# Opening of a two-layer encoder in a written order: low parts behind the next modulation, prompt's norm inside the first window of projections

## The chip, the cores and the metric

The kernel runs on one core of a Trainium2 chip. The metric is the device time of one execution in microseconds, the median of the runs shown.

## What is computed

Two token sequences, `sample` (512 tokens) and `prompt` (256 tokens), go through the same two layers with a model width of 1024. Each has its own conditioning vector `c`. The part that the change touches is the start of layer 0:

```python
def rmsnorm(x, g):
    xf = x.astype(jnp.float32)
    y = xf * lax.rsqrt(jnp.mean(xf * xf, axis=-1, keepdims=True) + EPS)
    return (y * g.astype(jnp.float32)).astype(x.dtype)
...
        mod = jax.nn.silu(c) @ adaln_w[l] + adaln_b[l]
        sh1, sc1, g1, sh2, sc2, g2 = [t[:, None, :] for t in jnp.split(mod, 6, axis=-1)]
        h = rmsnorm(x, norm_g[l, 0]) * (1 + sc1) + sh1
...
    proj = h @ w_in
```

`h` is projected onto the gates, queries, keys, values and output gates of a chunked mLSTM. Layer 1 has windowed attention in its place, and each layer ends with a convolutional feed-forward block. All matrix products are done to nearly full float32 precision.

## The kernel before

**Tiling.** Activations lie transposed: 8 chunks ("channels", `KC`) of 128 features on the partitions, 768 token columns. Columns 0 to 255 are prompt, 256 to 767 sample. `RANGES` cuts them into three ranges of 256 columns in the order sample, sample, prompt; `q` is 0 for sample and 1 for prompt.

**Split products.** A float32 operand becomes a high part (rounded to the type of one-pass products, by ScalarE, L232) and a low part (the rest, by VectorE, L233). A product is three products: high weight by high activation, high weight by low activation, low weight by high activation. Split activations live in `zh` and `zl` (also called `hh` and `hl`), split weights in `whi` and `wlo`, made from `raw`, a half unit of weights as loaded (128 x 1024). There are 5 buffers of `raw` and 3 each of `whi` and `wlo`.

**The opening.** `first` loads the x of the two sample ranges, computes the conditioning's first third (`adaln`, products of `silc` with rows of `adaln_w`) on TensorE and, meanwhile, the root mean squares of the two sample ranges (`Norm`, with `scaled` as what is done with the factors). Once shift and gain exist (L402, L405), `modulate` (L530 to L537) applies them to both ranges, channel by channel: gain and shift on VectorE (L534), then the split. `mlstm` then splits the first query weights, loads the x of prompt, squares it (L104, 8 tiles), and starts prompt's `Norm.stages`: first stage, sums over the squares by TensorE with two columns each (`pa<-inv,nt`, L120 region, recorded on the helper's line L226), epsilon on VectorE (L126), power on GpSimd (L127); second stage, factors spread over the partitions by TensorE (`pa<-kct,nr`), then `modulated` (L509): per channel a product on VectorE (L517), high part with shift on ScalarE (L519), low part on VectorE (L520).

**The window.** `window` (L283) takes three items (gates, first and second half of the first head's queries) and goes over the ranges in order; for each item it makes one tile of 24 products (8 channels by 3). After the second range, sample's results are evicted (`consume`: gates by L617 and L618, queries by L235 and L236), after the third, prompt's. `ready(rng)` makes sure that everything started for a range has been issued before the range is read; `tick` hands out dues of microseconds after which a started generator goes on.

**What sets the order.** The program is traced in the order of the code, and a planner reorders each engine's instructions by a simulated timeline. `manual_schedule(engines=...)`, used before only for the first feed-forward block, holds the instructions of its block on the named engines in traced order. DMAs are issued on SyncE's queue (SP). Passes for the conditioning of layer 1 (`adaln_v`, L474 and L476, tile `ada`) run on VectorE all through the mLSTM, as their rows arrive. After the window, the gates' rows go through logarithm and scans (L637 to L651), out to memory (`mrows`, L653) and back as masks and decays of the mLSTM.

Of the kernel before, what the change touches and what calls it, by code (L numbers as in the profile page):

```python
# [10 lines left out]
F32 = mybir.dt.float32  # L11
R = mybir.dt.float32r
AF = mybir.ActivationFunctionType
ALU = mybir.AluOpType
# [3 lines left out]
KC = D // P  # L18
# [4 lines left out]
SAMPLE, PROMPT = (256, 768, 0), (0, 256, 1)  # L23
RANGES = ((256, 512, 0), (512, 768, 0), PROMPT)
# [37 lines left out]
U_MIN = 0  # L62
# [22 lines left out]
class Norm:  # L85
# [11 lines left out]
    def x(self, c):  # L97
        return self.xt[c // 4][:, c % 4, self.rng[0] : self.rng[1]]
# [43 lines left out]
class Net:  # L142
# [137 lines left out]
            self.mm(o, wl[:, k], ah, False, k == KC - 1)  # L280
            yield o

    def window(self, items):  # L283

        bank = {}
        for rng in RANGES:
            self.ready(rng)
            c0, c1, q = rng
            s0, s1 = SEQS[q]
            for i, (w, consume) in enumerate(items):  # L290
                if (i, q) not in bank:
                    bank[i, q] = self.pa() if q else self.ps()
                wh, wl = (t.rearrange("p (k m) -> p k m", k=KC) for t in w)
                o = bank[i, q][:, c0 - s0 : c1 - s0]
                for k in range(KC):
                    ah, al = self.hh[:, k, c0:c1], self.hl[:, k, c0:c1]
                    self.mm(o, wh[:, k], ah, k == 0, False)
                    self.mm(o, wh[:, k], al, False, False)
                    self.mm(o, wl[:, k], ah, False, k == KC - 1)
                self.tick(2.6)  # L300
                if c1 == s1:
                    consume(q, bank[i, q][:, : s1 - s0])

    def gemmN(self, u, evac):

        ws = []
        for _, (hi, lo) in self.halves(u):
            ws.append((hi.rearrange("p (k m) -> p k m", k=4), lo.rearrange("p (k m) -> p k m", k=4)))
        for t in range(T // P):
            ps = self.ps()  # L310
            o = ps[:, :256]
            for k in range(KC):
                wh, wl = ws[k // 4]
                ah, al = self.hh[:, k, t * P : (t + 1) * P], self.hl[:, k, t * P : (t + 1) * P]
                self.mm(o, ah, wh[:, k % 4], k == 0, False)
                self.mm(o, al, wh[:, k % 4], False, False)
                self.mm(o, ah, wl[:, k % 4], False, k == KC - 1)
            evac(t, o)
# [208 lines left out]
            self.nc.vector.tensor_tensor(x(c), x(c), pr, ALU.mult)  # L527
        return ()

    def modulate(self, xt, rng, l, i):  # L530
        c0, c1, q = rng
        for c in range(KC):
            x = xt[c // 4][:, c % 4, c0:c1]
            self.nc.vector.tensor_scalar(  # L534
                x, x, self.gain[l][i][:, c, q : q + 1], self.mod[l][:, 24 * i + c, q : q + 1], ALU.mult, ALU.add
            )
            self.fp_copy_split(self.hh[:, c, c0:c1], self.hl[:, c, c0:c1], x)  # L537

    def output(self, x, pr, rng):
        nc = self.nc  # L540
# [63 lines left out]
    def mlstm(self, pool, gw, xt):  # L604
        nc, io = self.nc, self.io
# [14 lines left out]
        def keep(t, i, c):  # L620
            def evac(q, o):
                s0, s1 = SEQS[q]
                self.fp_copy_split(t[:, 0, c, s0:s1], t[:, 1, c, s0:s1], o, (1.0 / 16.0, None)[i])

            return evac

        qt0 = self.slab([P, 2, 2, T], R)
        ws = [(gw, gates)] + [(w, keep(qt0, 0, c)) for c, w in self.halves(U_MIN)]
        self.load_x(io["x"], RANGES[2:], xt)
        nc.sync.dma_start(self.kct[:, P:], io["kc"][:, P : 3 * P])  # L630
        norm = Norm(self, xt, PROMPT, self.modulated(0, 0), KC)
        for c in range(KC):
            norm.square(c)
        self.start(PROMPT, norm.stages())
        self.window(ws)
        nc.scalar.preload_act_table_set("natural_log_exp_and_others")
        nc.scalar.activation(ex, gf, AF.Abs)  # L637
        nc.scalar.activation(ex, ex, AF.Exp, scale=-1.0)
# [25 lines left out]
        for h in range(4):  # L664
# [48 lines left out]
            for q, (s0, s1) in enumerate(SEQS):  # L713
                n = (s1 - s0) // P
                for j in range(n):
# [7 lines left out]
                    w = (n + 1) * P  # L723
# [30 lines left out]
            for q, (s0, s1) in enumerate(SEQS):  # L754
                n = (s1 - s0) // P
                self.step(self.fillp, 2)
                hq = []
                for i in range(n):
# [5 lines left out]
                    for d in range(2):  # L764
                        o = self.pa()[:, :258]
                        js = range(0, i + 1) if d == 0 else range(i, n)
                        for j in js:
                            ph, pl = pts[q, j, d]
                            c0 = (i - j) * P if d == 0 else i * P
# [250 lines left out]
    def combined(self, l, i, pool):  # L1020
# [20 lines left out]
        def apply(x, pr, rng):  # L1041
            if rng[0] == 0:
                for c in range(KC):
                    full[c] = one(F32)
                    modulate(full[c], c, x, pr, rng)
                    put((self.B11, self.B21)[c // 4], c % 4, full[c])
                return
# [153 lines left out]
    def head(self, u0, last_tile, pool, urows, mark, early):  # L1201
# [48 lines left out]
        if not done:  # L1250
            self.fp_copy_split(*ahead[0], ah[0])
        first = self.outset(fixed(0), wa[0], rows[0][0])
        next(first)
        step()
        sums(1)
        wc[1] = self.split(ra[1])
        next(first, None)

        step()
# [181 lines left out]
    def first(self, pool):  # L1441

        x = self.io["x"]
        xt = self.load_x(x, RANGES[:1])
        ada = self.adaln(0, 0)
        steps = lambda n: [next(ada, None) for _ in range(n)]
        Norm(self, xt, RANGES[0], self.scaled).run()
        steps(4)
        self.load_x(x, RANGES[1:2], xt)
        steps(2)  # L1450
        Norm(self, xt, RANGES[1], self.scaled).run()
        self.graw = self.raw(self.io["wg"])
        steps(2)
        gates = self.split(self.graw)
        for rng in RANGES[:2]:
            self.modulate(xt, rng, 0, 0)

        def chain(*gens):
            for g in gens:
                yield from g  # L1460

        self.fillp = chain(*(self.adaln_g(0, grp) for grp in range(2, 6)))
        self.fill = self.adaln_v(1, pool)
        act = self.mlstm(pool, gates, xt)
        for _ in chain(self.fillp, self.fill):
            pass
        return act
# [129 lines left out]
```

## Time and profile before

| | |
|---|---|
| median of 3 runs | 1900.98 us (1899.35 to 1902.82) |
| the profiled execution's own time | 1904.33 us |
| its span in the profile | 1902.5 us |
| mean granted TensorE clock | 0.989 |
| TensorE busy | 1830.7 us, 96% of the span |
| VectorE, ScalarE, GpSimd busy | 1399.1, 910.3, 490.3 us |
| DMA | 184.48 MB, mean 97 GB/s |

PE is TensorE's products, PEld its weight loads, DVE VectorE, ACT ScalarE, POOL GpSimd, SP SyncE's queue. A row of the timeline gives start, duration, engine, line, operation, output and inputs, shape, count, and in brackets how long the engine was idle before and what released it. A busy TensorE is not TensorE at its peak: matmuls are pipelined, and their ends are modelled.

### The profile page before, as it was taken

What the parts mean: (1) busy time and instruction counts of PE and PEld (TensorE: products, weight loads), DVE (VectorE), ACT (ScalarE), POOL (GpSimd) and SP (SyncE); (2) the same over time, 40 slices, a digit from 0 to 9 for tenths busy, and PEclk for the clock granted to TensorE, in tenths of its full rate; (3) what the DMA queues carried; (4) which work ended last, traced back from release to release, by engine and by line L of the source; (5) the groups of instructions that cost most, each with busy time, mean ns of one, the idle gap of its engine ahead of it and who ended that gap; (6) DMA issues with size and microseconds to landing.
All of it is one profiled execution on the core that took longest, in us unless ns stands there. A gap on an engine that the chain in (4) does not pass through costs nothing. (4 is left out here: it accounts for less than half of the span.)

```text
span 1902.5 us, 29053 instructions
## 1 busy us (share of the span) xinstructions
PE 1830.7 (96%) x11270; PEld 1667.5 (88%) x11270; DVE 1399.1 (74%) x2296; ACT 910.3 (48%) x1832; POOL 490.3 (26%) x387
## 2 busy tenths in 40 slices
PE   7999999999999999999999999999989999999997
PEld 4987887888998999999999998779979999999997
DVE  4665577686689777777777755875997777777776
ACT  3444433444455444444444555774565444444443
POOL 2101001031023333333332211340133333333322
PEclk9999999999999999999999999999999999999998
DMA  8343556556312222222223221122222222222211
GB/s 330 109 134 121 167 181 195 168 164 208 99 53 69 68 67 67 67 67 67 67 67 100 90 89 43 44 85 89 78 78 78 67 67 67 67 67 67 67 34 67
DMA packets 64245, 184.48 MB, mean 97 GB/s; under 512 B 6167, under 2 KB 23831, under 8 KB 64108
## 3 DMA queue, kind: packets, MB, share of 16 engines
q1 hardware_dynamic: 64108, 182.63, 29.6%
q8 instruction: 88, 1.44, 0.3%
q14 instruction: 49, 0.40, 0.1%
HBM read 176.17 MB, written 6.43 MB: 96 GB/s over the span
## 5 line engine op out<-in xcount | busy, mean ns | idle before, releaser
L232 ACT CAST whi<-raw 128x1024 fp32r<-128x1024 f32 x237 | 248.5, 1049 | 412.2 <-PE pa L226 197.9
L233 DVE TENSOR_TENSOR wlo<-raw,whi 128x1024 fp32r<-128x1024 f32 x237 | 325.2, 1373 | 123.9 <-ACT whi L232 122.8
L226 PE MATMUL pa<-slab,whi 128*128 128x256 f32 (+1 forms) x1472 | 348.8, 334 | 4.7 <-DVE slab L557 4.5
L226 PEld LDWEIGHTS pa<-slab,whi 128*128 128x128 f32 x1472 | 254.0, 191 | 31.6 <-DVE slab L557 6.4
L557 DVE SCALAR_TENSOR_TENSOR slab<-pa,mod,slab 128x256 f32<-128x256 f32 (+1 forms) x368 | 207.6, 591 | 72.7 <-PE pa L226 72.3
L226 PE MATMUL pa<-slab,wlo 128*128 128x256 f32 (+1 forms) x736 | 235.4, 332 | 0.0
L226 PE MATMUL ps<-zh,whi 128*128 128x256 f32 (+2 forms) x688 | 228.8, 336 | 4.6 <-ACT whi L232 3.5
L226 PE MATMUL ps<-zh,wlo 128*128 128x256 f32 (+2 forms) x688 | 229.1, 336 | 4.0 <-DVE wlo L233 4.0
L226 PE MATMUL ps<-zl,whi 128*128 128x256 f32 (+2 forms) x688 | 229.4, 335 | 0.4 <-DVE zl L520 0.4
L1114 PE MATMUL ps<-zh,whi 128*128 128x384 f32 x504 | 171.1, 339 | 15.8 <-ACT ps L1169 14.5
L1115 PE MATMUL ps<-zl,whi 128*128 128x384 f32 x504 | 169.7, 337 | 0.8 <-DVE zl L1072 0.8
L1116 PE MATMUL ps<-zh,wlo 128*128 128x384 f32 x504 | 168.9, 335 | 0.0
L226 PEld LDWEIGHTS pa<-slab,wlo 128*128 128x128 f32 x736 | 140.2, 191 | 13.4 <-DVE wlo L233 0.9
L226 PEld LDWEIGHTS ps<-zh,whi 128*128 128x128 f32 x688 | 132.0, 193 | 17.5 <-ACT whi L232 5.1
L226 PEld LDWEIGHTS ps<-zh,wlo 128*128 128x128 f32 x688 | 132.2, 192 | 15.1 <-DVE wlo L233 4.8
L226 PEld LDWEIGHTS ps<-zl,whi 128*128 128x128 f32 x688 | 132.2, 193 | 11.5 <-issue 1.7
L1367 POOL TENSOR_TENSOR slab<-slab 128x772 f32<-128x772 f32 x44 | 83.7, 1903 | 205.0 <-DVE slab L1341 193.5
L1145 POOL TENSOR_TENSOR raw<-raw,raw 128x512 f32<-128x512 f32 x40 | 52.3, 1308 | 293.9 <-DVE wlo L233 244.3
L1340 DVE SCALAR_TENSOR_TENSOR slab<-slab,cstt,slab 128x771 f32<-128x771 f32 x88 | 104.8, 1193 | 26.9 <-ACT slab L1338 26.9
L1341 DVE SCALAR_TENSOR_TENSOR slab<-slab,cstt,slab 128x771 f32<-128x771 f32 x88 | 120.2, 1365 | 0.8
L476 DVE SCALAR_TENSOR_TENSOR ada<-raw,silc,ada 128x1024 f32<-128x1024 f32 x84 | 112.4, 1369 | 7.7 <-DMA raw<-in_adaln_w_dram 7.5
L1114 PEld LDWEIGHTS ps<-zh,whi 128*128 128x128 f32 x504 | 94.6, 188 | 23.9 <-ACT ps L1169 19.7
(291 smaller groups left out, 4155.0 us busy)
## 6 DMA issues: line engine op xcount, KB each, us to landing
raw<-in_w_dram SPq DMA_DIRECT2D x208, 512.0 KB, 3.7
raw<-in_adaln_w_dram SPq DMA_DIRECT2D x84, 512.0 KB, 4.3
slab<-in_x_dram SPq DMA_DIRECT2D x12, 512.0 KB, 7.6
slab<-in_adaln_w_dram SPq DMA_DIRECT2D x12, 512.0 KB, 10.3
slab<-mrows SPq DMA_DIRECT2D x8, 384.0 KB, 5.7
xs<-slab SPq DMA_DIRECT2D x6, 512.0 KB, 3.7
bt<-brow SPq DMA_DIRECT2D x16, 192.0 KB, 3.1
slab<-xs SPq DMA_DIRECT2D x6, 512.0 KB, 9.0
```

Source lines behind the costliest of these rows:

```text
L226: self.nc.tensor.matmul(out, lhsT, rhs, start=start, stop=stop)
L232: nc.scalar.copy(hi, src)
L233: return nc.vector.tensor_tensor(lo, src, hi.bitcast(F32), ALU.subtract)
L476: stt(acc[:, s], row, w, acc[:, s], ALU.mult, ALU.add)
L557: self.nc.vector.scalar_tensor_tensor(x, o, self.mod[l][:, gc + c, q : q + 1], x, ALU.mult, ALU.add)
L1114: mm(o, wh[:, k], hi[k], start=start and k == 0, stop=False, skip_group_check=True)
L1115: mm(o, wh[:, k], lo[k], start=False, stop=False, skip_group_check=True)
L1116: mm(o, wl[:, k], hi[k], start=False, stop=k == 3, skip_group_check=True)
L1145: tt(q[0], q[2], q[0], ALU.subtract)
L1340: stt(y[:, 1:], u[:, :-1], w(0), y[:, 1:], ALU.mult, ALU.add)
L1341: stt(y[:, :-1], u[:, 1:], w(2), y[:, :-1], ALU.mult, ALU.add)
L1367: nc.gpsimd.tensor_tensor(y, y, yrow[:, j], ALU.mult)
```

## The change

Prompt's norm and the window become one written section. `modulate` issues each channel's low part after the next channel's modulation, and calls `between(c)` after each high part: for the first range that is prompt's square of the same channel. The second range's modulation comes after the two weight splits. `window` takes prompt's stages: the sums are issued after the first tile, the factors and prompt's modulation after the fourth. The epsilon of prompt's mean is added by ScalarE (`last=True`, L124) instead of VectorE. TensorE, ScalarE and VectorE keep this order; SP and GpSimd are left to the planner. The other call of `window`, in layer 1, passes no stages.

```diff
--- before.py
+++ after.py
@@ -280,10 +280,16 @@
             self.mm(o, wl[:, k], ah, False, k == KC - 1)
             yield o
 
-    def window(self, items):
+    def window(self, items, stages=iter(())):
+
 
         bank = {}
+        n = 0
+        next(stages, None)
         for rng in RANGES:
+            if n == 2 * len(items):
+                for _ in stages:
+                    pass
             self.ready(rng)
             c0, c1, q = rng
             s0, s1 = SEQS[q]
@@ -300,6 +306,9 @@
                 self.tick(2.6)
                 if c1 == s1:
                     consume(q, bank[i, q][:, : s1 - s0])
+                n += 1
+                if n in (1, 4):
+                    next(stages, None)
 
     def gemmN(self, u, evac):
 
@@ -527,14 +536,21 @@
             self.nc.vector.tensor_tensor(x(c), x(c), pr, ALU.mult)
         return ()
 
-    def modulate(self, xt, rng, l, i):
+    def modulate(self, xt, rng, l, i, between=lambda c: None):
+
+        nc = self.nc
         c0, c1, q = rng
-        for c in range(KC):
-            x = xt[c // 4][:, c % 4, c0:c1]
-            self.nc.vector.tensor_scalar(
-                x, x, self.gain[l][i][:, c, q : q + 1], self.mod[l][:, 24 * i + c, q : q + 1], ALU.mult, ALU.add
-            )
-            self.fp_copy_split(self.hh[:, c, c0:c1], self.hl[:, c, c0:c1], x)
+        x = lambda c: xt[c // 4][:, c % 4, c0:c1]
+        for c in range(KC + 1):
+            if c < KC:
+                nc.vector.tensor_scalar(
+                    x(c), x(c), self.gain[l][i][:, c, q : q + 1], self.mod[l][:, 24 * i + c, q : q + 1], ALU.mult, ALU.add
+                )
+                nc.scalar.copy(self.hh[:, c, c0:c1], x(c))
+                between(c)
+            if c:
+                hi, lo = self.hh[:, c - 1, c0:c1], self.hl[:, c - 1, c0:c1]
+                nc.vector.tensor_tensor(lo, x(c - 1), hi.bitcast(F32), ALU.subtract)
 
     def output(self, x, pr, rng):
         nc = self.nc
@@ -625,14 +641,16 @@
             return evac
 
         qt0 = self.slab([P, 2, 2, T], R)
-        ws = [(gw, gates)] + [(w, keep(qt0, 0, c)) for c, w in self.halves(U_MIN)]
+        raws = [self.load(U_MIN, c) for c in range(2)]
         self.load_x(io["x"], RANGES[2:], xt)
         nc.sync.dma_start(self.kct[:, P:], io["kc"][:, P : 3 * P])
-        norm = Norm(self, xt, PROMPT, self.modulated(0, 0), KC)
-        for c in range(KC):
-            norm.square(c)
-        self.start(PROMPT, norm.stages())
-        self.window(ws)
+        norm = Norm(self, xt, PROMPT, self.modulated(0, 0), KC, last=True)
+        eng = mybir.EngineType
+        with self.tc.manual_schedule(engines={eng.PE, eng.Activation, eng.DVE}):
+            self.modulate(xt, RANGES[0], 0, 0, norm.square)
+            ws = [(gw, gates)] + [(self.split(raws[c]), keep(qt0, 0, c)) for c in range(2)]
+            self.modulate(xt, RANGES[1], 0, 0)
+            self.window(ws, norm.stages())
         nc.scalar.preload_act_table_set("natural_log_exp_and_others")
         nc.scalar.activation(ex, gf, AF.Abs)
         nc.scalar.activation(ex, ex, AF.Exp, scale=-1.0)
@@ -1452,8 +1470,6 @@
         self.graw = self.raw(self.io["wg"])
         steps(2)
         gates = self.split(self.graw)
-        for rng in RANGES[:2]:
-            self.modulate(xt, rng, 0, 0)
 
         def chain(*gens):
             for g in gens:
```

## The prediction

> **What bounds the kernel now.** The page of the profile comes first: the engines and the granted clock in 40 slices.
>
> ```profile
> PE 1830.7 (96%) x11270; PEld 1667.5 (88%) x11270; DVE 1399.1 (74%) x2296; ACT 910.3 (48%) x1832; POOL 490.3 (26%) x387
> PEclk9999999999999999999999999999999999999998
> ```
>
> TensorE holds 1830.7 of 1902.5 us; an edit of the opening pays only what it moves on TensorE's path, or what it moves on a chain TensorE later waits for. The change is in the first slice, 47.6 us long, and a little behind. So I cut that part into windows, then read it in order of time. The cut uses edges at which the granted clock changes (columns: length, busy time and count of PE, PEld, DVE, ACT, POOL, then clock, DMA share, GB/s):
>
> ```profile
> 34.79:38.20 3.41, 2.59 (x16) 1.95 (x15) 2.67 (x11) 2.96 (x10) 0.00 (x0) 1.00 1.03 410
> 38.20:41.61 3.41, 3.41 (x17) 3.41 (x17) 3.41 (x12) 3.41 (x10) 0.00 (x0) 0.50 0.88 350
> 41.61:45.03 3.42, 3.42 (x17) 3.42 (x18) 3.42 (x9) 3.30 (x9) 0.00 (x0) 0.50 0.05 18
> 45.03:48.44 3.41, 3.41 (x18) 3.41 (x18) 3.41 (x9) 0.00 (x0) 2.28 (x1) 0.50 0.51 154
> 48.44:51.85 3.41, 3.41 (x31) 3.41 (x31) 0.45 (x2) 0.00 (x0) 1.01 (x1) 1.00 0.46 154
> ```
>
> Half clock lasts from 38.20 to 48.44 us: 10.24 us, in which TensorE looks full. Timeline, TensorE:
>
> ```profile
> 25.09 1.50 PE L226 MATMUL pa<-inv,nt 128*128 128x2 f32 x12
> 35.37 1.30 PE L226 MATMUL pa<-inv,nt 128*128 128x2 f32 x8
> 36.84 0.38 PE L226 MATMUL ps<-zh,whi 128*128 128x256 f32 x1 [0.18 <-ACT zh L232]
> 37.87 5.16 PE L226 MATMUL pa<-inv,nt 128*128 128x2 f32 x24 [0.65 <-ACT nt L104]
> 42.89 0.56 PE L226 MATMUL ps<-zh,whi 128*128 128x256 f32 x1
> 44.53 0.41 PE L226 MATMUL ps<-zh,whi 128*128 128x256 f32 x1
> 45.17 0.41 PE L226 MATMUL ps<-zh,whi 128*128 128x256 f32 x1
> 51.27 0.60 PE L226 MATMUL pa<-kct,nr 128*128 128x128 f32 x4
> ```
>
> One product of the gates' tile runs at 36.84, then prompt's 24 remaining sums fill TensorE to 42.9; the rest of the 216 products follow. Prompt's factors slip in at 51.27. The three products of one channel take 45.17-44.53 = 0.64 us at half clock. VectorE, ScalarE and GpSimd in the same stretch:
>
> ```profile
> 26.86 0.72 POOL L127 TENSOR_TENSOR nr<-nr,mhalf 128x2 f32<-128x2 f32 x1 [1.83 <-DVE nr L126]
> 34.89 1.33 ACT L104 ACTIVATE nt<-slab 128x256 f32<-128x256 f32 x4
> 35.94 5.25 DVE L534 TENSOR_SCALAR slab<-slab,gain,mod 128x256 f32<-128x256 f32 x16
> 36.38 0.73 ACT L232 CAST zh<-slab 128x256 fp32r<-128x256 f32 x2 [0.16 <-DVE slab L534]
> 40.16 1.04 ACT L232 CAST whi<-raw 128x1024 fp32r<-128x1024 f32 x1
> 41.11 1.63 ACT L232 CAST zh<-slab 128x256 fp32r<-128x256 f32 x5
> 41.11 2.42 DVE L233 TENSOR_TENSOR zl<-slab,zh 128x256 fp32r<-128x256 f32 x7
> 43.46 1.21 DVE L233 TENSOR_TENSOR wlo<-raw,whi 128x1024 fp32r<-128x1024 f32 x1
> 46.16 3.29 POOL L127 TENSOR_TENSOR nr<-nr,mhalf 128x2 f32<-128x2 f32 x1 [18.59 <-DVE nr L126]
> 51.99 3.22 DVE L517 SCALAR_TENSOR_TENSOR nt<-slab,gain,pa 128x256 f32<-128x256 f32 x8 [3.10 <-issue]
> 52.50 3.31 ACT L519 ACTIVATE zh<-nt,mod 128x256 fp32r<-128x256 f32 x8 [7.59 <-DVE nt L517]
> 55.12 1.41 DVE L474 TENSOR_SCALAR ada<-raw,silc 128x1024 f32<-128x1024 f32 x2
> 56.45 3.25 DVE L520 SCALAR_TENSOR_TENSOR zl<-nt,mod,zh 128x256 fp32r<-128x256 f32 x8
> 57.43 0.69 ACT L617 ACTIVATE slab<-ps,cstt 36x512 f32<-36x512 f32 x1 [1.62 <-PE ps L226]
> 60.31 0.60 ACT L235 ACTIVATE slab<-ps 128x512 fp32r<-128x512 f32 x1 [1.49 <-PE ps L226]
> 60.45 2.48 DVE L476 SCALAR_TENSOR_TENSOR ada<-raw,silc,ada 128x1024 f32<-128x1024 f32 x2 [0.75 <-DMA raw<-in_adaln_w_dram]
> 63.19 0.60 ACT L235 ACTIVATE slab<-ps 128x512 fp32r<-128x512 f32 x1 [2.28 <-PE ps L226]
> 66.94 0.47 ACT L617 ACTIVATE slab<-pa,cstt 36x256 f32<-36x256 f32 x1
> ```
>
> Before, the planner runs all 16 modulations, then the low parts; and for prompt 8 products in a row, then the 8 low parts together. The tile evictions (57.43, 60.31, 63.19) show the pace of a tile of 24 products at full clock: 2.88 us, 0.36 per channel. Prompt's first tile thus starts at about 63.0 and ends at 65.9, unhindered: its last low part was done at 59.7.
>
> **First range and prompt's sums.** No instruction is added but one form of it: the epsilon goes from VectorE to ScalarE. The rest is order. VectorE now alternates modulation (5.25/16 = 0.33 us) and low part (2.42/7 = 0.35): 0.67 a channel. ScalarE alternates high part (1.63/5 = 0.33) and prompt's square (1.33/4 = 0.33): 0.66. From 36.38 the first channel, then seven steps of 0.67: the eighth low part ends near 41.8, and the gates' first tile on TensorE ends near 42.1. At half clock its products need 0.64 a channel, so VectorE is still the pace and the clock costs nothing here. Then the 32 sums stand alone on TensorE: 1.50/12 = 0.125 us each, 4.0 us, to 46.1. So 7.0 us of sums that lay over the modulation become 4.0 us that lie over nothing, and a tile of 2.9 takes their place; in exchange the products are no longer started at half clock.
>
> The two weight splits follow the first range on both engines (1.04 and 1.21 each): high parts 42.7 and 43.7, low parts 43.9 and 45.1, ahead of 46.1. The second range's modulation takes 8 x 0.67 = 5.4 us, to about 51. TensorE needs it from 46.1 + 2 x 2.88 = 51.9: hidden with 0.9 us to spare. The mean's epsilon now waits on ScalarE behind the last high part (50.7), and the power takes 0.72 us on GpSimd with VectorE idle, or up to 3.29 with VectorE busy as at 46.16: 51.4 to 54.0, against a need at 54.7. It is hidden, and its cover is thin. SP's queue gets the same loads in the same traced order: two weight halves, x of prompt, constants. I price that at nothing: the squares of before ran from 34.89 on, those of the written order from 36.7.
>
> **The fourth tile and prompt's factors.** The fourth tile's eviction falls at 46.1 + 3 x 2.88 = 54.7, against 57.43: 2.7 us ahead. The factors cost 0.6 on TensorE now instead of earlier: 2.1 ahead. Two tiles later, at 61.0, TensorE is at prompt's first tile, 2.0 us ahead of 63.0.
>
> But prompt's modulation starts only now, and in written order: product, high part, low part, next product. ScalarE first runs the gates' two evictions (0.69 for the one in the row above, L618's the same shape; to 56.1), which are queued ahead of the high parts. A channel then costs 0.51 from product to high part (51.99 to 52.50), 0.51 for a high part by itself (3.31 less seven steps of 0.40), and 0.40 from low part to next product (3.25/8): an estimate of 1.42 us. The first low part starts at 56.7, the eighth at 56.7 + 7 x 1.42 = 66.6 and ends at 67.1 (3.25 less seven steps is 0.45); the tile ends at 67.4. Unhindered it would have ended at 61.0 + 2.9 = 63.9: a wait of 3.5 us on TensorE is added, split over the last channels, with prompt's two other tiles queued behind it, and 2.0 ahead becomes 1.5 behind (65.9). Also behind that chain stand the evictions of the second and third sample tile, on ScalarE and VectorE; the banks that they free are wanted only after prompt's tiles. Below that, the price is nothing only if the low parts don't follow the written order (a rival below).
>
> Whether passes of the other layer's modulation (ada) slip into VectorE's gaps, the trace tells: an outsider does run inside a written section of the first feed-forward block, since L1340 stands ahead of L1317 of the section:
>
> ```profile
> 566.89 2.98 DVE L1340 SCALAR_TENSOR_TENSOR slab<-slab,cstt,slab 128x771 f32<-128x771 f32 x2
> 570.72 0.55 DVE L1317 TENSOR_TENSOR slab<-pa,nt 128x384 f32<-128x384 f32 x1
> ```
>
> The gap is 0.53 us; one of the two at 55.12 (0.7) costs 0.2, one of those at 60.45 (1.24) costs 0.7: 0 to 1.8 us for all four. I take 0, since the rows land when they do and VectorE is idle from 51 to 55, where the first pair fits.
>
> **What follows the opening.** These rows show who waits next:
>
> ```profile
> 85.82 0.38 SPq L653 DMA_DIRECT2D mrows<-slab  x1
> 88.81 0.43 SPq L241 DMA_DIRECT2D raw<-in_w_dram  x1
> 88.91 0.39 PE L226 MATMUL ps<-whi,zh 128*128 128x256 f32 x1 [0.46 <-DVE slab L233]
> 96.63 1.05 ACT L232 CAST whi<-raw 128x1024 fp32r<-128x1024 f32 x1 [7.75 <-DMA raw<-in_w_dram]
> 99.33 0.39 PE L226 MATMUL ps<-whi,zh 128*128 128x256 f32 x1 [1.52 <-DVE slab L233]
> ```
>
> A weight load at 88.81 stands on SP behind the gates' rows (85.82), these behind the scans, these behind prompt's gates (66.94): so the gates' date, and not TensorE's own lateness, sets 99.33. That tile ended at 65.9, and its eviction came 1.0 later, behind a weight split on ScalarE; that split (one of 1.04, like 40.16) becomes ready as the gates' tile ends. In the new order the date is 67.4 without it and 68.4 with it: 0.5 to 1.5 us later. I take 1.2, nearer the upper end, since the planner of before put the split first.
>
> **The clock.** The sums are work of two columns. In 38.20 to 41.61 they filled TensorE by the record (3.41 of 3.41) and the clock stayed at 0.50; it came back only after 45.03 to 48.44, which held products alone. The stretch that ended with half clock (34.79 to 38.20) held mostly such sums. So 4.0 us of sums between 42.1 and 46.1 may put the clock down again. If it drops as they end and one stretch of 3.41 us of products brings it back, the loss is 3.41/2 = 1.7 us; if it drops inside them, two stretches pass: 3.4 us; if an edge falls in their middle, both neighbours hold about half products: 0. I take the middle, 1.7.
>
> [...]
>
> The sum: +1.2 for the gates' date and +1.7 for the clock, +2.9 us on the profiled execution's 1904.33 (span 1902.5). That execution is 3.35 above the median of the runs, 1900.98; the difference goes onto the median: 1903.9 us. Its own bounds: 0.5 to 1.5 and 0 to 3.4, with ada 0 to 1.8, so +0.5 to +6.7.
>
> **The rivals.** *The clock stays up* (small sums count as work): the clock term is 0, +1.2 us, 1902.2. For it: 25.09, where twelve sums ran 0.125 each at full clock; against it: the 38.20 row. Within 0.2% as well.
>
> *The clock goes down for two stretches.* One mechanism: an edge of the windows falls in the last 1.5 us of the sums (44.5 to 46.1), half clock holds from there over the stretch that is part sums and over one whole stretch of products. Price 3.4 in place of 1.7, and the gates' tile ends after the split at the late end, 1.5: +4.9 us, 1905.9. With the edges of this execution (45.03) it is exactly this case. It decides as soon as the loss passes 3.8 - 1.2 = 2.6 us. One ada pair in the chain (1.4) does the same to a middle clock term.
>
> *The order isn't what is written, and the stage behind is planned anew.* If prompt's products still run first (3.22 in a row), the chain is short, the 2.0 us ahead stay; with the clock up and the load of 88.81 put ahead of the rows, the waits of 0.46 and 1.52 vanish too: -4.0 us, 1897.0. For it: a planner that orders by expected dates redoes everything after the opening. Against it: three conditions at once.
>
> **How the numbers follow.** 0.2%, 3.8 us, is about what a measurement of this kernel can tell from no change. Forecast (+2.9; its own range 1902 to 1904.8) 0.36, clock up 0.07, two stretches 0.35, planned anew and faster 0.22. Same is 0.43, slower 0.35, faster 0.22. The range takes the faster rival's 1897.0 as its low end, half of that case outside, and 1908.0 at the top (+6.7 is 1907.7): one in ten outside at each end.
>
> **What would show it.** Right: gates' first tile from 36.8 to about 42 at 0.66 a channel; 32 sums in one block behind it, some 4 us; prompt's VectorE row alternating L517 and L520 every 1.4 us or more; a TensorE wait of some 3.5 us in prompt's first tile on zl; its gates' eviction at 68 to 71; a second stretch of half clock between 43 and 52. Wrong: no such wait, or the full clock throughout after 41.6, or a difference that arises behind 100 us, by another order of loads and splits.

## The result, and the profile after

The changed kernel took 1910.82 us (median of 6 runs, 1907.03 to 1914.85) beside 1900.16 us for the kernel before (6 runs): a ratio of 1.0058, with a 95% interval of 1.004 to 1.0075. That is 10.7 us slower, and above the top of the predicted range (1908.0). A second set of six runs gave 1910.21 and 1.0054 (1.0036 to 1.0072).

The profiled execution took 1909.49 us, with a span of 1907.7. The page, engines and clock:

```profile
PE 1833.3 (96%) x11270; PEld 1667.3 (87%) x11270; DVE 1403.8 (74%) x2295; ACT 912.4 (48%) x1833; POOL 483.8 (25%) x387
PEclk9899999999999999999999999999999999999998
```

TensorE's busy time grew by 2.6 us, the span by 5.2. Only the second slice of the clock, 48 to 95 us, looks different. Windows of the profile after, cut at the edges at which the clock changes (columns as in the prediction):

```profile
37.79:41.21 3.42, 3.42 (x16) 3.34 (x16) 3.29 (x11) 3.42 (x12) 0.00 (x0) 0.51 0.97 387
41.21:44.62 3.41, 3.41 (x32) 3.40 (x31) 2.58 (x4) 1.92 (x3) 0.00 (x0) 1.00 0.14 25
44.62:48.03 3.41, 3.41 (x18) 3.41 (x18) 3.26 (x10) 1.94 (x5) 0.00 (x0) 0.50 0.85 275
48.03:51.44 3.41, 3.41 (x18) 3.41 (x18) 2.45 (x7) 0.68 (x2) 0.00 (x0) 0.50 0.05 22
...
65.09:68.51 3.42, 2.26 (x8) 1.25 (x8) 2.07 (x5) 1.17 (x3) 0.00 (x0) 1.00 0.24 93
68.51:71.92 3.41, 2.74 (x7) 1.69 (x7) 1.88 (x5) 1.50 (x4) 0.00 (x0) 0.50 0.00 0
71.92:75.34 3.42, 3.42 (x15) 3.18 (x16) 2.91 (x5) 3.25 (x6) 0.00 (x0) 0.50 0.00 0
75.34:78.75 3.41, 3.41 (x30) 3.41 (x30) 0.43 (x1) 3.36 (x4) 0.00 (x0) 1.00 0.51 159
```

Before, half clock ended at 48.44 and did not return in the opening. Now there are three spells: 3.4 us in the gates' first tile, 6.8 us from 44.62, the last part of the sums, on, and 6.8 us more, from 68.5, in prompt's tile: 17.1 us in place of 10.2. The stretch ahead of the third holds eight products (65.09).

TensorE's timeline after:

```profile
36.47 0.38 PE L226 MATMUL ps<-zh,whi 128*128 128x256 f32 x1 [1.36 <-ACT zh L549]
41.78 4.26 PE L226 MATMUL pa<-inv,nt 128*128 128x2 f32 x32
57.03 0.60 PE L226 MATMUL pa<-kct,nr 128*128 128x128 f32 x4
64.55 0.38 PE L226 MATMUL pa<-zh,whi 128*128 128x256 f32 x1 [0.43 <-ACT zh L528]
66.01 0.38 PE L226 MATMUL pa<-zh,whi 128*128 128x256 f32 x1 [0.43 <-ACT zh L528]
...
79.73 0.40 PE L226 MATMUL ps<-zh,whi 128*128 128x512 f32 x1
```

The 32 sums stand in one block. In prompt's first tile a product waits for each channel, 1.45 us apart. The last row is the first product with 512 columns behind the window, a mark that all kernels here share. In the kernel before it stands here:

```profile
71.63 0.40 PE L226 MATMUL ps<-zh,whi 128*128 128x512 f32 x1
```

The mark is 8.1 us later. VectorE after the change (L526 and L529 are the L517 and L520 of before, prompt's product and low part; L485 is the L476 of before, a pass of layer 1's conditioning):

```profile
49.06 1.42 DVE L483 TENSOR_SCALAR ada<-raw,silc 128x1024 f32<-128x1024 f32 x2 [0.96 <-DMA raw<-in_adaln_w_dram]
54.32 2.48 DVE L485 SCALAR_TENSOR_TENSOR ada<-raw,silc,ada 128x1024 f32<-128x1024 f32 x2 [1.63 <-DMA raw<-in_adaln_w_dram]
57.72 0.48 DVE L526 SCALAR_TENSOR_TENSOR nt<-slab,gain,pa 128x256 f32<-128x256 f32 x1 [0.92 <-issue]
59.04 0.48 DVE L529 SCALAR_TENSOR_TENSOR zl<-nt,mod,zh 128x256 fp32r<-128x256 f32 x1 [0.83 <-ACT zh L528]
59.44 0.47 DVE L526 SCALAR_TENSOR_TENSOR nt<-slab,gain,pa 128x256 f32<-128x256 f32 x1
60.69 2.48 DVE L485 SCALAR_TENSOR_TENSOR ada<-raw,silc,ada 128x1024 f32<-128x1024 f32 x2 [0.77 <-DMA raw<-in_adaln_w_dram]
63.09 0.48 DVE L529 SCALAR_TENSOR_TENSOR zl<-nt,mod,zh 128x256 fp32r<-128x256 f32 x1
63.48 0.47 DVE L526 SCALAR_TENSOR_TENSOR nt<-slab,gain,pa 128x256 f32<-128x256 f32 x1
...
64.94 0.47 DVE L526 SCALAR_TENSOR_TENSOR nt<-slab,gain,pa 128x256 f32<-128x256 f32 x1
65.99 0.48 DVE L529 SCALAR_TENSOR_TENSOR zl<-nt,mod,zh 128x256 fp32r<-128x256 f32 x1 [0.58 <-ACT zh L528]
...
71.80 0.48 DVE L529 SCALAR_TENSOR_TENSOR zl<-nt,mod,zh 128x256 fp32r<-128x256 f32 x1 [0.58 <-ACT zh L528]
```

Each low part waits 0.58 us for its high part, and the next product stands behind it. At 60.69 two ada passes have taken the gap between a product and its low part, 2.48 us long: from that product to the next are 4.04 us (59.44 to 63.48) in place of 1.46 (63.48 to 64.94). ScalarE, GpSimd and SP (L633 is the L617 of before, the gates' eviction; L671 its L653, the gates' rows):

```profile
52.38 0.87 POOL L127 TENSOR_TENSOR nr<-nr,mhalf 128x2 f32<-128x2 f32 x1 [25.18 <-ACT nr L124]
57.22 0.68 ACT L633 ACTIVATE slab<-ps,cstt 36x512 f32<-36x512 f32 x1 [4.92 <-PE ps L226]
73.95 0.47 ACT L633 ACTIVATE slab<-pa,cstt 36x256 f32<-36x256 f32 x1
92.77 0.37 SPq L671 DMA_DIRECT2D mrows<-slab  x1
```

Prompt's gates are evicted at 73.95, against 66.94: 7.0 us later. The rows follow at 92.77, 6.95 later.

Product by product, in the times of before, the profile after is behind by 8.0 us at 80, 5.1 at 120 to 140, 4.3 at 160 to 250, 7.1 around 300, 5.8 around 500, 6.2 at 1100 and 7.9 at 1800. The first part of the loss comes back where TensorE waited before: 2.3 us in three waits between 80 and 120, none of which is left. The profile of before then has a half-clock spell of 6.8 us at 1881 that the one after lacks, and the spans differ by 5.2. The order of the instructions behind the opening is nearly the same in both. The median gap of 10.7 is those 5.2, plus 4.2 by which the profiled execution of before was above the median of that set, plus 1.3 by which the one after was below its own.

### The profile page after: what moved, and what is told of

It is laid out like the page before. It is cut to its first block, busy times and chain, and to the rows that moved or that the text cites. A ratio compares the mean times of both kernels' runs of the same rounds, so it can differ in the third digit from the quotient of the medians.

```text
span 1907.7 us, 29049 instructions
## 1 busy us (share of the span) xinstructions
PE 1833.3 (96%) x11270; PEld 1667.3 (87%) x11270; DVE 1403.8 (74%) x2295; ACT 912.4 (48%) x1833; POOL 483.8 (25%) x387
## 5 line engine op out<-in xcount | busy, mean ns | idle before, releaser
L233 DVE TENSOR_TENSOR wlo<-raw,whi 128x1024 fp32r<-128x1024 f32 x237 | 331.8, 1401 | 122.3 <-ACT whi L232 121.1
L485 DVE SCALAR_TENSOR_TENSOR ada<-raw,silc,ada 128x1024 f32<-128x1024 f32 x84 | 108.9, 1326 | 7.6 <-DMA raw<-in_adaln_w_dram 7.5
```

Source lines behind the costliest of these rows:

```text
L233: return nc.vector.tensor_tensor(lo, src, hi.bitcast(F32), ALU.subtract)
L485: stt(acc[:, s], row, w, acc[:, s], ALU.mult, ALU.add)
```

## The experiments

Two theories stood at the start: the loss lies in the opening, as prompt's chain on VectorE and ScalarE, ada passes inside it and the clock's answer to the block of sums; or it arises behind it, by another plan of loads and splits. "Mark" below is the first product of 512 columns in the profiled execution; times are medians, and ratios are to the kernel before in the same set of runs. Where an expectation has a name for what sets the clock, the runs show of it the granted clock alone: 1.00 or 0.50, with edges on a grid of 3.41 us (last section).

**The changed kernel again.** No edit.

> The changed kernel once more, so that the experiments beside it are compared on one chip, and to see a second profiled execution. Theory (written chain and clock): the same picture in the opening, a wait of TensorE in prompt's first tile of about 5 us, half clock once around the sums and once in prompt's first tile, and a ratio of 1.004 to 1.007 to the kernel before. Rival (the 10.7 us of the medians are mostly an accident of the executions): a ratio near 1.003, as the one pair of profiles gives (1909.49 against 1904.33).

1910.21 us, mark 80.33, the same three half-clock spells 0.6 us later. The loss and its picture repeat.

**Prompt's low parts one channel behind.** In `modulated`:

```diff
+            late = []
...
-                nc.vector.scalar_tensor_tensor(lo, t, sh, hi.bitcast(F32), ALU.add, ALU.subtract)
+                late.append((lo, t, sh, hi.bitcast(F32), ALU.add, ALU.subtract))
+                if l or c:
+                    nc.vector.scalar_tensor_tensor(*late.pop(0))
+            for args in late:
+                nc.vector.scalar_tensor_tensor(*args)
```

> Prompt's low parts stand one channel behind the products in the written order, nothing else is changed. Theory (the strictly alternating chain of product, high part, low part holds up prompt's first tile): VectorE takes 0.8 us a channel instead of 1.45, the eighth low part ends near 65.5 instead of 72.3, prompt's first tile runs without a wait and near 66 its eviction begins, the half clock of 68.5 to 75.4 is gone, and TensorE is 6 to 8 us earlier behind the opening: a ratio of 1.000 to 1.002. Rival (the loss arises behind the opening, by another order of loads and splits): the opening is shorter, but the ratio stays at 1.004 or more.

1905.59 us, ratio 1.0026 (1.0015 to 1.0037). The timeline and one window of this kernel (an ada pair on VectorE, TensorE's wait, the window of prompt's tile, the mark):

```profile
62.05 2.48 DVE L485 SCALAR_TENSOR_TENSOR ada<-raw,silc,ada 128x1024 f32<-128x1024 f32 x2
66.56 0.39 PE L226 MATMUL pa<-zl,whi 128*128 128x256 f32 x1 [0.16 <-DVE zl L532]
65.08:68.50 3.42, 2.94 (x20) 2.31 (x19) 3.24 (x9) 2.29 (x5) 0.00 (x0) 1.00 0.51 153
74.89 0.40 PE L226 MATMUL ps<-zh,whi 128*128 128x512 f32 x1
```

A channel takes 0.79 us on VectorE, TensorE's waits fall to 0.16, the stretch at 65 holds 20 products in place of 8, and the half clock in prompt's tile is gone. The mark is 4.8 us earlier, although the first modulation came 1.3 us later in this execution (36.90 against 35.56); the median is 4.6 lower. An ada pair still stands in the chain (62.05), and the ratio is above the 1.000 to 1.002 that the theory gave. Of the causes tried singly, the low part that waits for its own channel's high part is the largest.

**The ada passes behind prompt's last low part.**

```diff
+                self.low = nc.vector.scalar_tensor_tensor(lo, ...)
...
-                        self.step(self.fill)
+                        with self.tc.issue_after(self.low.ins):
+                            self.step(self.fill)
```

> The passes for layer 1's conditioning that the planner slid into the section are queued behind prompt's last low part; the order of the section is kept as it is. Theory (the alternating chain, with the pair of passes of 2.48 us at 60.7 as its smaller part): the eighth low part ends some 2.5 us earlier, TensorE is 2.5 us earlier behind the opening, the wait in prompt's first tile stays at about 3 to 4 us: a ratio of 1.003 to 1.005. Rival (the pair of passes is what breaks the chain, and the alternation alone would be hidden): most of the loss goes, a ratio under 1.002.

1908.46 us, ratio 1.004 (1.0025 to 1.0056). The gates' eviction comes at 71.82, 2.1 earlier than after; the mark at 78.59, 1.1 earlier. So the pair does lie on the chain, but much of it is lost again by the mark. The intervals of the two kernels overlap, and its worth in time is not resolved.

**The sums in two halves,** 16 behind the first tile and 16 behind the second.

```diff
                 net.mm(pm[:, 2 * b : 2 * b + 2], ...)
+            if self.written and b < nb - 1:
+                yield 0.0
...
-                if n in (1, 4):
+                if n in (1, 2, 4):
...
+        norm.written = True
```

> Prompt's sums stand in two halves: 16 behind the first tile, 16 behind the second, instead of 32 behind the first; nothing else is changed. Theory (a stretch of 3.4 us that is mostly sums puts the clock down): with blocks of 2.1 us each stretch holds products for a third or more of its time, the clock stays up from 41 to 52, and the fourth tile is evicted 3.4 us earlier, near 53.8; the chain behind it moves with it, a ratio 0.0015 to 0.002 below that of the changed kernel. Rival (the clock comes back only after a fixed stretch of dense products from the start, however the sums stand): half clock from 44.6 to 51.6 as before, and the ratio of the changed kernel.

1914.36 us, ratio 1.0072 (1.0055 to 1.0089): by the medians slower than the kernel it was to mend, with overlapping intervals. The timeline of this kernel (L488 is the ada pass, L529 prompt's product, L636 the gates' eviction):

```profile
42.44 1.84 PE L229 MATMUL pa<-inv,nt 128*128 128x2 f32 x16
47.10 1.84 PE L229 MATMUL pa<-inv,nt 128*128 128x2 f32 x16
54.82 0.68 ACT L636 ACTIVATE slab<-ps,cstt 36x512 f32<-36x512 f32 x1 [2.14 <-PE ps L229]
55.67 2.48 DVE L488 SCALAR_TENSOR_TENSOR ada<-raw,silc,ada 128x1024 f32<-128x1024 f32 x2 [2.60 <-DMA raw<-in_adaln_w_dram]
58.07 0.47 DVE L529 SCALAR_TENSOR_TENSOR nt<-slab,gain,pa 128x256 f32<-128x256 f32 x1
61.64 2.48 DVE L488 SCALAR_TENSOR_TENSOR ada<-raw,silc,ada 128x1024 f32<-128x1024 f32 x2 [0.18 <-DMA raw<-in_adaln_w_dram]
```

The clock stays up from 42.1 to 66, and the fourth tile is evicted at 54.82, 2.4 earlier than after and where the prediction had put it. But the ada pair that came at 54.32 in the changed kernel comes at 55.67, now ahead of prompt's first product, and another stands within the chain. The gates' date is 73.45, the mark 79.85: the 2.4 us ended at a chain that did not move. The time is about 4 us above the changed kernel's, and a good part of that can be half clock: the granted clock is 0.9868 in the mean of these runs (each is listed to 0.001) against 0.9882 in those of the changed kernel beside them, 2.5 us if TensorE had work in all of it. The profile has longer spells (10.2 us at 66 and again at 151) and more of them behind 690. What brings them was not tested.

**The three together.** All three edits.

> The three edits together: low parts one channel behind the products in prompt's modulation, sums in two halves behind the first and second tile, the passes for layer 1's conditioning behind prompt's last low part. Theory (chain, passes and clock make up the loss in the opening): no wait in prompt's first tile, full clock from 42 on, the fourth tile evicted near 54.8, prompt's gates near 64 to 65 instead of 73.95, and the first 512-column product near 69.7, against 71.63 in the kernel before; a ratio of 0.998 to 1.000 if nothing else moves. Second theory (later waits of some 2 us, at the same places in every kernel, cost a half-clock stretch of 3.41 us, or 1.7 us of time, whenever one falls whole into a window of the monitor; a shifted opening chooses other hits): the opening as above, but the ratio anywhere from 0.997 to 1.004, with the difference to the opening's made up of half-clock stretches behind 100 us. Rival (another order of work behind the opening): a difference behind 100 us without half-clock stretches.

> The three changes together once more (low parts of prompt one channel behind, sums in two halves, layer 1's passes behind the last low part), as the base for the two kernels run beside it. Both theories expect what it gave: about 1900.7 us, ratio 1.000 to 1.002, the first product of 512 columns near 69 us, and half clock after the wait of 1.87 us near 676, because there the wait falls whole into one of the gate's stretches of 3.41 us.

1900.72 us, ratio 1.0008 (0.9999 to 1.0016), and in the second set 1901.12 us, 1.0016 (1.0005 to 1.0028). The mark is 68.91 and 69.54, ahead of the kernel before by 2.7 and 2.1. Mark and loss of the lead in the first set's profile:

```profile
68.91 0.40 PE L229 MATMUL ps<-zh,whi 128*128 128x512 f32 x1
87.55 0.84 ACT L779 ACTIVATE slab<-slab 36x768 f32<-36x768 f32 x1 [7.88 <-DVE slab L723]
88.92 2.75 PE L229 MATMUL pa<-slab,slab 128*128 128x512 f32 x6 [2.68 <-ACT slab L235]
```

Nearly all of the loss is undone by edits of the opening, so it came from there. The lead is gone by 90 us: TensorE waits 2.68 us for ScalarE's casts, which stand behind a step on the gates' rows (L779, at 87.55, before 86.81) that VectorE releases, and half clock follows at 89.2. Neither theory nor the rival had this wait. In the second set the profile has no half clock at 680, with a wait of 2.54 us in place of 1.87 and other edges: that spell is not a property of the kernel.

**The block alone.** The first two edits, the sums in one block.

> The three changes together but for the sums, which stay in one block behind the first tile: prices the block alone. Theory (the block puts the clock down for two stretches, 6.83 us at half speed, on TensorE's path): half clock from 44 or so to 51, the fourth tile's eviction near 57 in place of 54.3, the first product of 512 columns 3.4 us later, near 72.3, and 3 us on the time where later stretches are the same: 1902 to 1905. Rival (the loss is absorbed by prompt's chain, which has its own pace): the fourth tile late by 2.9, but the product of 512 columns near 70 and the time within 1 us of the base.

1904.28 us, ratio 1.0027 (1.0016 to 1.0038), 3.2 above the base of the same set. Windows and timeline of this kernel:

```profile
41.40:44.82 3.42, 3.42 (x32) 3.38 (x31) 2.59 (x4) 2.02 (x3) 0.00 (x0) 1.00 0.07 22
44.82:48.23 3.41, 3.41 (x17) 3.41 (x18) 3.26 (x11) 1.95 (x5) 0.00 (x0) 0.50 0.93 288
48.23:51.65 3.42, 3.42 (x18) 3.42 (x18) 2.23 (x7) 1.29 (x4) 0.87 (x1) 0.50 0.04 14
72.18 0.40 PE L226 MATMUL ps<-zh,whi 128*128 128x512 f32 x1
```

Half clock for two stretches, and the mark 2.6 to 3.3 later than with halves, near the 3.4 us that two half-clock stretches cost (6.83 us at a granted clock of 0.50): in the opening the block has that price when nothing slower stands behind it. On the time it is less sure: 3.2 us by the medians, 2.1 by the ratios, and the intervals overlap.

**No written window.** Only the modulations and splits are held in order; prompt's stages are started as before.

```diff
-            self.window(ws, norm.stages())
+        self.start(PROMPT, norm.stages())
+        self.window(ws)
```

> Only the modulations and weight splits stay a written section; prompt's stages are started as in the kernel before, and the planner places sums, factors and prompt's modulation around the window's tiles. Theory (the written places of prompt's norm are the fault, not the alternating modulation): half of the sums lie between the channels of the first tile, prompt's products stand eight in a row, no wait in prompt's first tile, at most one stretch of half clock after 41, and the first 512-column product near 67 to 69 against 71.63 before and 79.73 in the changed kernel; the ratio is below that of the changed kernel by 0.003 or more, 0.997 to 1.001 before later hits of the clock. Rival (the section itself, that is its modulations, is the fault): the ratio stays at 1.004 or more.

1902.0 us, ratio 1.0012 (1.0 to 1.0025). The planner puts 14 of the sums between the products of the first tile and the rest in two blocks behind it; half clock holds from 37.3 to 54.4, five stretches, and the mark is 75.17, not 67 to 69. Yet the median is below those of kernels with an earlier mark (1905.59 us with 74.89, 1904.28 with 72.18). One of its windows:

```profile
40.73:44.15 3.42, 3.42 (x18) 3.42 (x18) 2.45 (x6) 3.30 (x7) 0.00 (x0) 0.50 0.11 43
```

The ratio says that the written places of prompt's norm make most of the loss, and the written modulations alone do not. The mark is a guide to the opening, not a price in the total to the last 3 us.

**The kernel before, started later:** 14 small VectorE steps ahead of its first modulation.

```diff
+                for _ in range(7):
+                    g = self.gain[l][0][:, :, s]
+                    nc.vector.tensor_scalar(g, g, 1.0, None, ALU.mult)
```

> The kernel before with its opening held up: 14 small steps on VectorE, each multiplying the gains by one, stand between the gains and the first modulation, some 1.7 us, half a window of the clock's monitor; the order of work behind it is the same but for some 140 rows of 13643. Theory of the hits (where a wait falls against the monitor's windows decides over 1.7 us each): the opening is 1.7 later, and the median moves by something else than 1.7, from -3 to +7 us, by half-clock stretches that come or go at the known places (about 150, 260 or 320, 420, 690, 1050, 1390, 1610 us). Rival (only the opening counts): the median moves by 1.5 to 2 us and the same stretches are there.

1899.38 us, ratio 1.0001 (0.9991 to 1.001). The first modulation came at 37.63 in place of 35.94, 1.7 us later, and the mark at 71.67, where before had 71.63. Half clock in the opening lasted 6.83 us in place of 10.24, which would give back 1.7; the sums also ran ahead of the first product here, so the clock's part is not separated. A later start of everything is not by itself a cause of the loss.

**The kernel before, one more look.** No edit.

> The kernel before once more, for a second profiled execution. Theory of the hits: the opening is the same within 0.5 us, half clock near 38 to 48 again; the list of later half-clock stretches may differ from the first execution's (147, 318, 417, 1048, 1881 us), and the difference of the spans is 1.7 us for each stretch of 3.41. Rival: the same list, and spans that differ for another reason.

1901.2 us (one run), mark 70.84, the same opening. The later half-clock spells differ: those near 145 and 415 are there, 3.4 us longer each, there is one at 682, and there is none at 318, 1048 or 1881.

**The three together, started later.** The 14 steps of above.

> The three changes together, with 14 small VectorE steps (about 1.5 us) ahead of the first modulation, so that everything behind stands 1.5 us later against the gate's stretches, whose edges do not move with the work. Theory (a later wait costs a stretch of half clock only where it lies whole between two edges): the wait of 1.87 us near 678 now stands across an edge, 1.6 to 3.5 behind the last one, and the half clock at 680 is gone; with that 1.7 is won back, so the time is within 1 us of the base although the opening is 1.5 later (first product of 512 columns near 70.4). Rival (the half clock behind that wait has nothing to do with where it falls): the same stretches as the base at 680, 1045 and 1386, each 1.5 later, and the time 1.5 above it.

1903.07 us, ratio 1.002 (1.001 to 1.003), 2 above the base by the medians, with overlapping intervals. Windows around the wait near 680, first the three together, then this kernel, cut at each one's own edges:

```profile
676.31:679.72 3.41, 1.54 (x9) 1.51 (x9) 1.08 (x2) 2.63 (x5) 1.13 (x1) 0.99 0.27 111
679.72:683.13 3.41, 3.41 (x12) 3.41 (x12) 1.79 (x2) 0.48 (x1) 0.15 (x1) 0.51 0.30 74
```

```profile
678.99:682.40 3.41, 2.91 (x17) 2.59 (x15) 3.13 (x4) 1.70 (x3) 0.00 (x0) 1.00 0.83 225
682.40:685.82 3.42, 2.05 (x12) 2.05 (x13) 1.09 (x2) 2.63 (x5) 1.29 (x1) 1.00 0.19 77
685.82:689.23 3.41, 3.41 (x19) 3.23 (x19) 1.78 (x4) 1.58 (x3) 0.00 (x0) 1.00 0.49 143
```

The same wait of 1.87 us lies within one stretch above (1.54 busy, half clock follows) and across an edge below (2.91 and 2.05 busy, none follows), as its theory said. But the time did not come back: the mark is 71.38, and a spell at 256 is new in this profile (one at 1048 stands in both). The intervals overlap, so on the time neither side is shown.

**The lead kept.** The three together end the opening 2.7 us ahead of before, but send the gates' rows at 86.56 (before: 85.82), since an ada pair ran ahead of the scans. Here it is held behind the last scan (`last`).

```diff
-                        with self.tc.issue_after(self.low.ins):
+                        with self.tc.issue_after((last if t == 4 else self.low).ins):
```

> The three changes together, whose opening is 2.7 us ahead of the kernel before at the first product of 512 columns, but whose gates' rows go out at 86.6 us, behind the 85.8 of before: a pair of ada passes (2.47 us) has come ahead of the gates' scans on VectorE. Here that pair is held behind the last scan. Theory (the lead is lost to that pair): rows out near 84.1, 1.7 ahead of before, and 1.5 to 2.5 us off the time of the base, 1898.5 to 1899.5, ratio 0.999. Rival (the lead is lost in the wait of 3.5 to 3.9 us near 141 and in half clock behind it, whatever the rows' date): rows out at 84.1 as well, but the time stays at 1900.5 to 1901.5.

The rows of the three together, then of this kernel:

```profile
72.88 2.47 DVE L488 SCALAR_TENSOR_TENSOR ada<-raw,silc,ada 128x1024 f32<-128x1024 f32 x2
86.56 0.38 SPq L680 DMA_DIRECT2D mrows<-slab  x1
```

```profile
83.32 2.48 DVE L488 SCALAR_TENSOR_TENSOR ada<-raw,silc,ada 128x1024 f32<-128x1024 f32 x2
83.32 0.38 SPq L680 DMA_DIRECT2D mrows<-slab  x1
85.72 0.94 DVE L778 TENSOR_TENSOR slab<-slab 36x768 f32<-36x768 f32 x1
```

The rows go out 3.2 us earlier, and the time is no better: 1905.63 us, ratio 1.0027 (1.0014 to 1.0041), spread from 1899.5 to 1909.6. The theory falls: the lead was not lost to the rows' date alone. The pair now stands ahead of VectorE's next step on the gates' rows (L778), so ScalarE's step behind that comes at 86.70 in place of 87.55, only 0.85 earlier, and TensorE still waits, 3.22 us at 89.68. The profiled execution, at 1899.53, is the fastest of the twelve. The others are slower in good part by half clock: the granted clock is 0.9877 in the mean of the runs against 0.9896 in those of before beside them, 3.6 us if TensorE had work in all of it, of 4.7. Which waits bring it, no profile shows. No version of the change beats the kernel before.

## Why the prediction was wrong

The step that failed is the gates' date. The sum gave it 1.2 us, and it came 7.0 us later (66.94 to 73.95), because the ada passes were put at nothing (2.6 us measured) and because the chain was dated at full clock, with the clock's loss added as a term of its own (on the chain, 2.3 us by the late fourth tile and some 0.7 at its end). The clock term knew only the spell at the sums; there was a second one in prompt's tile.

**What held.** The gates' tile began at 36.47 and ran at 0.66 us a channel; the sums stood in one block behind it, 4.26 us against 4.0, ending at 46.0 against 46.1. The power took 0.87, hidden. (The "7.0 us of sums" of before are 1.30 and 5.16 in the rows, 6.5; nothing in the sum hangs on it.) The order was the written one, and prompt's chain had its 1.45 us a channel (1.42 predicted), with TensorE waiting in prompt's tile. That tile stood on ScalarE's high parts rather than on `zl`, as the waits are recorded. The order behind the opening hardly changed. So the rival of a new plan, given 0.22, did not occur.

**The clock term.** The sum took 1.7 us, the middle of 0 to 3.4. The stretches 44.62 and 48.03 are those of the rival of two stretches, with the edge in the last 1.5 us of the sums, as it asked for, and the block alone cost 2.6 to 3.3 us at the mark. The fourth tile is evicted at 57.22 in place of 54.7. 41.21 to 44.62 is full by the record (3.41 of 3.41), at full clock, and half clock follows it: as from 38.20 to 41.61 in the kernel before, a stretch of sums that the record shows as full had no full clock behind it.

**The second clock loss.** That the waits in prompt's tile could themselves bring the clock down was in no step, not even in the range. At 1.45 us a channel a stretch holds eight products (65.09), where one of products alone holds 30 (75.34), and two stretches at half clock follow. They lie partly beside the chain; what they cost alone was not measured. The low parts moved one channel behind took most of the waits and this half clock away together, 4.6 us.

**Ada at nothing.** The step that put 0 to 1.8 us for the ada passes, and took 0, priced each pass by what it overhangs a gap of 0.5 us of its own. Here two passes stood in one gap, 2.48 us long, and put the chain back by 2.6 (4.04 less 1.46), more than the bound of 1.8 for all four. The step had placed the first pair in VectorE's idle time from 51 to 55; the pairs came at 49, 54 and 60.7, as their rows landed.

**The gates' date.** Predicted 67.4 to 68.4, measured 73.95. From the 68.1 of the sum (66.94 and 1.2) these are 5.8 us: 2.3 by the first low part (59.04 in place of 56.7, behind the fourth tile's lateness), 2.6 by the ada pair, 0.2 by 1.45 against 1.42 over seven channels, and 0.7 left behind the last low part, in half clock. The mechanism (a later date, carried to the rows) was right; its inputs were too small, because the date was summed with the clock up, the clock added elsewhere, and the ada pair left out; all three act in series on one chain.

**From opening to total.** Opening and total agree only to a few us. At the mark the loss is 8.1 us; the three edits that undo it take the ratio from 1.0058 to 1.0008 or 1.0016. Between the two profiled executions the loss is 5.2, inside the forecast's own bounds of 0.5 to 6.7; that is luck, as the one of before was 4.2 above the median of its set. Half clock is the smaller part: the granted clock is 0.9882 in the mean of the second set's runs of the changed kernel against 0.9900 in those of before, 3.5 us if TensorE had work in all of it, of 9.9. How the rest behind the opening arises is not settled. Part of it is half clock behind waits of 0.9 to 2 us (in the kernel before 1.90 us up to 317.96 and 0.93 up to 1046.92, after the change 1.69 up to 258.50), which appears at 255, 318, 415, 680, 1048, 1390 or 1610 in one profile and not in the next, so that no single pair of profiles gives the price of an edit of this size.

## What to carry to other kernels

Before a chain of product, high part and low part is written out in order, count what a channel costs when the low part waits for its own high part: one channel of lag took it from 1.45 to 0.79 us. An order written on some engines leaves gaps that the planner fills with whole work of its own size: price a gap at the length of the longest ready outsider, not of the gap. And a wait on TensorE can have a second price, the clock (here two stretches at 0.50 behind one that held eight products): look at what each 3.41 us stretch will hold, in the stage that is thinned as well as in the one that is moved.

## What the runs showed of the hardware

Half-clock spells start and end at whole multiples of 3.41 us from the first edge, all through an execution, but for the last, which the end cuts: in the profile of before they start 32, 82, 111, 296, 540 and 544 stretches behind the first, in that of after 2, 9, 33, 65, 113, 298 and 545. The waits do not set the edges, they only fall among them. One wait of 1.87 us was enough where it lay within one stretch, as the windows near 680 show: with the low parts alone (1.54 us busy from 679.47 to 682.88) and with the three together (1.54 from 676.31 to 679.72) half clock follows. Where an edge cuts the wait, none follows: in the kernel before 1.87 us, with 3.02 and 1.93 busy on the two sides of 683.31; in the three started later 1.87, with 2.91 and 2.05; in the changed kernel 2.54, with 2.27 and 2.02 on the two sides of 689.71.

Busy time by the record does not tell what the clock does. 16 sums and the 16 products beside them in a stretch kept the clock up (the sums at 42.44, in halves), 26 sums with six products put it down (41.21), and eight products of 256 columns with 2.26 us of record put it down (65.09) where 12 products of 384 columns with 2.05 us did not (682.40). These would agree if the clock went by the columns that stream (256 in a product of 128x256, 2 in a sum): 4128 and 4608 where it stayed up, 1588 and 2048 where it went down. The profiles of before and after lean that way: of their 1069 stretches at full clock from 35 us on, 13 have half clock behind them, and sorted by columns (a product that an edge cuts counted by its share) all but 2 fall on the right side of one limit, sorted by busy time all but 6. One of the 2 is a stretch of products with smaller weights (128*32, at 146.99 after the change). It is a sorting after the fact; no run changed the columns alone, so what the clock goes by is not shown.
